# A tile of h in two VectorE operations, the next tile's product ahead of the last low part, first loads on one queue, and factors in the statistic's bank

## The chip, the cores and the metric

One NeuronCore of a Trainium2 chip runs the whole program. The metric is device time in microseconds (us) for one execution, as a median over runs. A profiled execution gives the trace. Its span, from the first to the last instruction, is a little shorter than its device time. In the profile PE is the tensor engine (PEld its weight loads), DVE is VectorE, ACT is ScalarE, POOL is GpSimd and SP is the engine that issues most of the DMAs.

## The reference: what is computed

Two layers of a decoder trunk over 512 tokens of 1024 channels, fp32 in and out. Layer 0 mixes tokens with stick-breaking attention (16 heads of 64), layer 1 with a diagonal state-space layer. After each comes a gated MLP (2 x 2816 channels) with a causal convolution of width 3. Ahead of each of these four parts stands an RMS norm whose gain and shift depend on a vector c:

```python
def rms_norm(x, g):
    y = x * lax.rsqrt(jnp.mean(x * x, axis=-1, keepdims=True) + EPS)
    return y * g

mod = silu(c) @ w_mod[i] + b_mod[i]              # 6 * 1024 numbers for a layer
sh1, sc1, g1, sh2, sc2, g2 = split(mod, 6)
h = rms_norm(x, norm_mix[i]) * (1 + sc1) + sh1   # "a tile of h" is 128 channels of this
y = attention(h)                                 # layer 0: q, k, v = split(h @ w_qkv, 3), ...
x = x + g1 * y
h = rms_norm(x, norm_ffn[i]) * (1 + sc2) + sh2
x = x + g2 * conv_ffn(h)
```

At the end stands one more such norm. In the kernel's names a tile k of h is `x[k] * rstd * a[k] + b[k]`, with `a` the gain and `b` the shift (a number for each channel, so for each partition) and `rstd` the factor of each token.

## The kernel before, in words

Channels lie on partitions and tokens along the free axis: x is eight tiles of 128 x 512. Every matrix product is made with about fp32 accuracy out of three products in a rounded format: each operand is split into a high part (rounded) and a low part (the rest), and PE makes high x high, high x low and low x high. ACT makes the high part (a copy that rounds) and DVE the low part (a difference). Weights arrive by DMA in pieces of 128 x 1024 (512 KB) in a rotating set of three raw buffers (`wraw`), and are split into a rotating set of five pairs (`wH`, `wL`).

The numbers of `mod` are products of rows of w_mod with silu(c): DVE multiplies a 128 x 1024 piece by `cact` and adds up each partition (`gemv_step`, L195), one instruction for one column of 128 numbers. Columns (1, k) are the gain of tile k and columns (0, k) its shift. The 16 columns that layer 0's first norm needs go through four slots (`slot`, `wload`, `wnext`); the others are spread over the kernel as background work.

A planner (`schedule_with_timeline_sim`) orders the instructions of each engine; `pe_pin` and `keep_in_program_order` keep the ones that they mark in the order of the code, and `follow` puts an instruction behind the last one of a line for its engine. In the first stage nearly everything is pinned.

The first stage (`attention`, the part before the score products) goes as follows.

1. First loads. `xload(0, G)`, small and `xload(1, G)` go through POOL's queue; c, the columns of w_mod, w_v and the other tiles of x through SP's.
2. v is computed before the norm's statistic is known. PE multiplies `x[k] * a[k]` (`xa_high`, `xa_low`) with w_v, and the factor of each token is applied when v leaves PSUM (`v_evict`, with the factors `yv`). v is eight banks: tiles 0 to 3 are four groups of 128 tokens for the first 512 channels, 4 to 7 the same for the second. The shift `b` can't be put in that way, so it is carried by the last token's column (`LAST`): it gets the shift instead (`shift_high`, `shift_low`), and later stages take differences of neighbouring tokens. Tiles 3 and 7 (`vz`) hold that column and wait for the shift; the six others (`va`) don't. For k below `KLATE` = 5 the products of `vz` come later, for k = 5 to 7 all eight tiles go together.
3. While this runs, squares of x are added up (`square`, `add`). After tile 7 PE sums over channels (the bank `stat`), ACT takes the root, five small DVE operations give the factors `y`. ACT and POOL make four diagonal blocks `dg` of them, and PE spreads the factors over the partitions, into a second bank (`rbc`). A copy of it is `rb`.
4. Then h itself is made, tile by tile, with `norm_tile`: on DVE `t = x * rb` (L305), on ACT the high part `a * t + b` rounded (L312) and the same affine unrounded (L314), on DVE the difference of the two (L318). Tile 0 is made between the products of k = 6 and k = 7, the others behind all of v. Evictions of v (three on DVE, `VDVE`, five on ACT) and the splits of the first k and q weights (`qk_split`) stand between the tiles.
5. PE makes k and q of head pair 0 from h, six products for each tile, then the same for pair 1, and begins with the scores (z) of pair 0. v goes out to DRAM (`sV`) and is read back one token shifted (`vs`); `v_diff` takes the difference.

A Sigmoid table is loaded on ACT, by a small activation `warm`, behind the last eviction (L805).

`norm_tile` is used three more times by way of `head_mm` (the two MLPs and the state-space layer): there in halves of 256 tokens for tiles 0 to 5 and whole for tiles 6 and 7, with the factors read from PSUM, while PE multiplies each tile with four weights at once.

Of the kernel before, what the change touches and what calls it, by code (L numbers as in the profile page):

```python
# [16 lines left out]
P = 128  # L17
# [24 lines left out]
VDVE = (1, 4, 6)  # L42
# [49 lines left out]
def _trunk(ctx, tc, I, out, tap):  # L92
# [205 lines left out]

    def norm_tile(h, k, bc, a, b, cr=FULL, pinned=False, first=None, mid=None):
        n = cr.stop - cr.start  # L300
        t = np_.tile([P, T], F32, tag="nt1", bufs=2, name="nt1")[:, :n]
        u = np_.tile([P, T], F32, tag="nt2", bufs=1, name="nt2")[:, :n]
        for part in HALF if cr == FULL and isinstance(bc, dict) else (cr,):
            src = bc[part.start] if isinstance(bc, dict) else bc
            pin["nt"] = V.tensor_tensor(t[:, part.start - cr.start:part.stop - cr.start], x[k][:, part], src[:, part], ALU.mult)  # L305
        hh, hl = h[0][k][:, cr], h[1][k][:, cr]
        hf = hh.bitcast(F32)
# [4 lines left out]
        act = S.activation(hh, t, AF.Identity, bias=b[:, k:k + 1], scale=a[:, k:k + 1])  # L312
        keep(act)
        aff = S.activation(u, t, AF.Identity, bias=b[:, k:k + 1], scale=a[:, k:k + 1])  # L314
        keep(aff)
        if mid:
            mid()
        dve = V.tensor_tensor(hl, u, hf, ALU.subtract)  # L318
        keep(dve)
        pin["head"].append([act, aff, dve])  # L320
# [218 lines left out]
    def attention(acc):  # L539
        with ExitStack() as av_, ExitStack() as ac:  # L540
# [20 lines left out]
            def xload(k, queue=SP):  # L561
                pe_pin(queue.dma_start(x[k], I["xT"][k * P:(k + 1) * P, :]))
# [24 lines left out]
            pe_pin(V.scalar_tensor_tensor(ab, sm("b_mod", mcol(0, 1, 0)), 1.0, sm("norm_mix", 0), ALU.add, ALU.mult))  # L587
# [79 lines left out]
            for i in va:  # L667
                vb[i] = bank(name=f"v{i}")
            high(0, 0)
            gv(1, 0)  # L670
            gain(0)
            xa_high(0)
            low(0, 0)
            high(0, 1)
# [4 lines left out]
            for q in TERMS:  # L679
                for half in (va[:3], va[3:]):  # L680
                    prods(0, half, (q,))
            for k in range(1, 4):
                high(k)
                gv(1, k)
                gain(k)
                xa_high(k)
                for q in (2 * k - 2, 2 * k - 1):
                    if q:
                        add(q)
                low(k)  # L690
                xa_low(k)
                for q in (2 * k, 2 * k + 1):
                    square(q)
                if k < 3:
                    prods(k, va)
            prods(3, va[:4])
            for q in (6, 7):
                add(q)
# [6 lines left out]
            prods(3, va[4:])  # L705
            high(4)
            gv(1, 4)
            nv, nsd, y, ntm = (np_.tile([P, 4], F32, tag=g, bufs=2, name=g) for g in ("nv", "nsd", "ny", "ntm"))
            pe_pin(S.activation(nsd, st[:, :4], AF.Sqrt, bias=epst, scale=1.0 / D))
            gain(4)  # L710
            xa_high(4)
# [5 lines left out]
            low(4)  # L717
            xa_low(4)
            for i in range(4):
                dst = R["dg"][:, i * P:(i + 1) * P]  # L720
                if i < 2:
                    pe_pin(S.activation(dst, ident, AF.Copy, scale=y[:, i:i + 1]))
                else:
                    G.tensor_scalar(dst, ident, y[:, i:i + 1], 0.0, ALU.mult, ALU.add)
# [7 lines left out]
            prods(4, va[:4])  # L732
            rbp = bank(aux, "rbc")
            for cr in HALF:
                pe_pin(PE.matmul(rbp[:, cr], ones, R["dg"][:, cr], start=True, stop=True))
            rb = np_.tile([P, T], F32, tag="sq", bufs=2, name="rb")
            pe_pin(S.activation(rb, rbp, AF.Copy))
            prods(4, va[4:])
            gv(0, 0)
            for i in vz:  # L740
                vb[i] = bank(aux, f"v{i}")
# [7 lines left out]
            def norm(k):  # L749
                norm_tile(h, k, rb, a, b, FULL, True)  # L750

            for k in range(KLATE, KD):
                high(k)
                gv(1, k)
                gain(k)
                xa_high(k)
                low(k)
                xa_low(k)
                gv(0, k)
                shift_high(k)  # L760
                shift_low(k)
                prods(k, va + vz)
                if k == KD - 2:
                    norm(0)
# [4 lines left out]
            def v_evict(i):  # L769
                nb, tt = divmod(i, 4)  # L770
                dst = vn[:, tt, nb * 512:(nb + 1) * 512]
                if i in VDVE:
                    pe_pin(V.tensor_scalar(dst, vb[i], yv[:, tt:tt + 1], None, ALU.mult))
                else:
                    pe_pin(S.activation(dst, vb[i], AF.Copy, scale=yv[:, tt:tt + 1]))
# [9 lines left out]
            def qk_split(nm):  # L785
                (wh, wl), qkr = qkw[0, nm]
                pe_pin(S.activation(wh, qkr, AF.Copy))
                pe_pin(V.tensor_tensor(wl, qkr, wh.bitcast(F32), ALU.subtract))
                qkw[0, nm] = wh, wl

            last_load = pin["load"]
# [10 lines left out]
            line["S"], line["V"] = pin["head"][-1][1:]  # L802
# [190 lines left out]
            for pr in range(2):  # L993
                if pr == 0:
                    for nm in QK:
                        qk_load(1, nm, True)

                    todo = []
                    units = proj(0, todo)
                    for k in range(KD):  # L1000
                        units[k]()
                        units[KD + k]()
                    for evict in todo:
                        evict()
                    for i in (1, 2, 5, 6, 3, 7, 0, 4):
                        v_diff(i, follow)
# [713 lines left out]
```

## Time and profile before

| what | before |
|---|---|
| median of 3 runs | 1197.9 us (1197.64 to 1198.16) |
| profiled execution | 1201.34 us |
| its span | 1199.3 us |
| mean granted TensorE clock | 0.996 |
| PE busy | 1164.9 us |
| DVE busy | 859.0 us |
| ACT busy | 568.8 us |
| POOL busy | 273.5 us |
| bytes moved by DMA | 211.52 MB, mean 176 GB/s |

How to read it: a row such as `62.40:93.56 31.16, 21.70 (x72) ...` gives a stretch of the span in us, its length, and for PE, PEld, DVE, ACT and POOL the busy time and the number of instructions, then the granted clock, the share of time in which the DMA engines were busy, and GB/s. A row of a timeline gives start, duration, engine, line, operation, output and inputs; in brackets stands how long the engine was idle before it and what ended that. A row of waits gives total, times and the longest one. In a row of a group the numbers behind the bar are the busy time, the mean ns of one instruction and the idle time before them. Engine times overlap, so that only a wait on the chain to the end costs time.

### The profile page before, as it was taken

What the parts mean: (1) busy time and instruction counts of PE and PEld (TensorE: products, weight loads), DVE (VectorE), ACT (ScalarE), POOL (GpSimd) and SP (SyncE); (2) the same over time, 40 slices, a digit from 0 to 9 for tenths busy, and PEclk for the clock granted to TensorE, in tenths of its full rate; (3) what the DMA queues carried; (4) which work ended last, traced back from release to release, by engine and by line L of the source; (5) the groups of instructions that cost most, each with busy time, mean ns of one, the idle gap of its engine ahead of it and who ended that gap; (6) DMA issues with size and microseconds to landing.
All of it is one profiled execution on the core that took longest, in us unless ns stands there. A gap on an engine that the chain in (4) does not pass through costs nothing.

```text
span 1199.3 us, 16512 instructions
## 1 busy us (share of the span) xinstructions
PE 1164.9 (97%) x6196; PEld 955.8 (80%) x6196; DVE 859.0 (72%) x1322; ACT 568.8 (47%) x902; POOL 273.5 (23%) x282
## 2 busy tenths in 40 slices
PE   8969999999999999999999999999999999999997
PEld 6747778679788888878888887879888888888887
DVE  6758988877799658676867598787598467744555
ACT  6466566656453134412435677645544134422443
POOL 1100111000097799979820000000000000000003
PEclk9989999999999999999999999999999999999999
DMA  9644555451157757779745598772176338442222
GB/s 362 249 158 158 158 181 162 132 183 48 49 163 250 251 167 228 225 241 296 236 144 179 180 347 275 237 238 64 51 227 211 123 118 193 145 123 71 82 77 71
DMA packets 91507, 211.52 MB, mean 176 GB/s; under 512 B 19586, under 2 KB 37778, under 8 KB 91428
## 3 DMA queue, kind: packets, MB, share of 16 engines
q1 hardware_dynamic: 78676, 192.56, 49.7%
q0 software_dynamic: 4432, 15.82, 4.2%
q10 hardware_dynamic: 8320, 2.10, 0.8%
q8 instruction: 48, 0.79, 0.3%
q14 instruction: 31, 0.25, 0.1%
HBM read 189.20 MB, written 21.24 MB: 175 GB/s over the span
## 4 chain that ended last, share of the span: by engine, by line
PE 74%; DVE 8%; issue 7%; DMA 6%; ACT 4%; POOL 1%; POOLq 0%; DVEq 0%; ACTq 0%; SPq 0%
PE up L168 13%; PE up L171 13%; PE up L172 13%; PE dn L168 6%; PE dn L171 6%; PE dn L172 6%; DMA wg<-in_w_modT_dram 3%; PE u L171 1%; PE u L168 1%; PE u L172 1%; PE wos L171 1%; PE v L661 1%; PE wo L168 1%; PE wos L172 1%; PE wo L172 1%
## 5 line engine op out<-in xcount | busy, mean ns | idle before, releaser
L168 PE MATMUL up<-hH,up_h 128*128 128x512 f32 x640 | 249.7, 391 | 0.3 <-DVE ca L458 0.3
L172 PE MATMUL up<-hH,up_l 128*128 128x512 f32 x640 | 249.2, 389 | 0.3 <-DVE up_l L163 0.3
L171 PE MATMUL up<-hL,up_h 128*128 128x512 f32 x640 | 249.2, 389 | 0.0
L458 DVE SCALAR_TENSOR_TENSOR ca<-up,small,ca 128x511 f32<-128x511 f32 (+1 forms) x176 | 131.6, 748 | 118.9 <-ACT ca L456 115.9
L168 PE MATMUL dn<-gH,dn_h 128*128 128x512 f32 (+1 forms) x394 | 146.5, 373 | 0.0
L172 PE MATMUL dn<-gH,dn_l 128*128 128x512 f32 (+1 forms) x394 | 146.0, 370 | 0.0
L171 PE MATMUL dn<-gL,dn_h 128*128 128x512 f32 (+1 forms) x394 | 145.8, 370 | 0.0
L195 DVE SCALAR_TENSOR_TENSOR wg<-wg,cact 128x1024 f32<-128x1024 f32 x96 | 120.7, 1274 | 31.7 <-DMA wg<-in_w_modT_dram 31.7
L168 PEld LDWEIGHTS up<-hH,up_h 128*128 128x128 f32 x640 | 120.1, 188 | 26.6 <-issue 1.7
L172 PEld LDWEIGHTS up<-hH,up_l 128*128 128x128 f32 x640 | 120.1, 188 | 25.7 <-DVE up_l L163 0.8
L171 PEld LDWEIGHTS up<-hL,up_h 128*128 128x128 f32 x640 | 120.1, 188 | 24.3
L456 ACT ACTIVATE ca<-up,small 128x512 f32<-128x512 f32 x88 | 68.1, 774 | 148.3 <-PE up L172 148.3
L1592 POOL TENSOR_SCALAR xa<-x,Anorm_out 128x256 f32<-128x256 f32 x7 | 5.7, 817 | 575.2 <-DVE x L352 575.2
L162 ACT ACTIVATE up_h<-up_r 128x1024 fp32r<-128x1024 f32 x80 | 84.2, 1053 | 79.7 <-PE dn L171 57.6
L163 DVE TENSOR_TENSOR up_l<-up_r,up_h 128x1024 fp32r<-128x1024 f32 x80 | 113.8, 1423 | 7.6 <-ACT up_h L162 6.8
L352 DVE SCALAR_TENSOR_TENSOR x<-dn,mod,x 128x512 f32<-128x512 f32 (+1 forms) x55 | 37.5, 681 | 79.7 <-PE dn L172 79.5
L168 PEld LDWEIGHTS dn<-gH,dn_h 128*128 128x128 f32 x394 | 73.9, 188 | 14.8 <-issue 0.6
L172 PEld LDWEIGHTS dn<-gH,dn_l 128*128 128x128 f32 x394 | 73.9, 188 | 14.2
L171 PEld LDWEIGHTS dn<-gL,dn_h 128*128 128x128 f32 x394 | 73.9, 188 | 14.2
L162 ACT ACTIVATE dn_h<-dn_r 128x1024 fp32r<-128x1024 f32 (+1 forms) x48 | 46.7, 982 | 50.5 <-PE dn L171 43.3
L474 ACT ACTIVATE gH<-gm 128x512 fp32r<-128x512 f32 x44 | 27.1, 616 | 69.8 <-DVE gm L470 69.8
L163 DVE TENSOR_TENSOR dn_l<-dn_r,dn_h 128x1024 fp32r<-128x1024 f32 (+1 forms) x48 | 59.2, 1234 | 0.4
(356 smaller groups left out, 2330.9 us busy)
## 6 DMA issues: line engine op xcount, KB each, us to landing
up_r<-in_w_up_dram SPq DMA_DIRECT2D x80, 512.0 KB
wg<-in_w_modT_dram SPq DMA_DIRECT2D x74, 512.0 KB
dn_r<-in_w_down_dram SPq DMA_DIRECT2D x32, 512.0 KB
wg<-in_w_modT_dram POOLq DMA_DIRECT2D x22, 512.0 KB, 3.8
wgs<-in_w_modT_dram SPq DMA_DIRECT2D x16, 512.0 KB
dn_r<-in_w_down_dram SPq DMA_DIRECT2D x16, 384.0 KB
wv_r<-in_w_v_dram SPq DMA_DIRECT2D x8, 512.0 KB
wk_r<-in_w_qk_dram SPq DMA_DIRECT2D x8, 512.0 KB
```

Of the source, the lines that this page charges most:

```text
L162: order("S", lambda: S.activation(wh[:, :n], raw[:, :n], AF.Copy))
L163: pin["split"] = order("V", lambda: V.tensor_tensor(wl[:, :n], raw[:, :n], wh[:, :n].bitcast(F32), ALU.subtract))
L168: ins = PE.matmul(ps, ah, bh, start=start, stop=False)
L171: PE.matmul(ps, ah, bl, start=False, stop=False)
L172: PE.matmul(ps, al, bh, start=False, stop=stop)
L195: mul = lambda: V.scalar_tensor_tensor(w, w, 1.0, cact, ALU.mult, ALU.mult, accum_out=raw[:, col:col + 1])
L352: add = lambda: V.scalar_tensor_tensor(xs, pv, gate, xs, ALU.mult, ALU.add)
L456: follow("S", lambda: S.activation(ca, ps, AF.Identity, bias=small[:, cb:cb + 1], scale=tapw[2]))
L458: follow("V", lambda: V.scalar_tensor_tensor(ca[:, q:], ps[:, :T - q], tapw[2 - q], ca[:, q:], ALU.mult, ALU.add))
L474: follow("S", lambda: S.activation(gh, m, AF.Copy))
L661: pe_pin(PE.matmul(vb[i], h[p_][k][:, tt * P:(tt + 1) * P], wv[k][q][:, nb * 512:(nb + 1) * 512], start=k == 0 and (p_, q) == (0, 0), stop ...
L1592: G.tensor_scalar(xa[k], x[k][:, cb], a[:, k:k + 1], 0.0, ALU.mult, ALU.add)
```

## The change

- `norm_tile` (all four places): the product takes the gain with it, `t = (x * a) * rstd`, one DVE instruction of the three-operand form; ACT makes one pass for the high part, `t + b` rounded; the low part is `(t + b) - high`, one DVE instruction. The unrounded affine on ACT and its buffer are gone.
- The first norm is taken out of the v loop and written as a loop of its own (`nt_mul`, `nt_high`, `nt_low`): the product of tile k + 1 stands on DVE ahead of the low part of tile k. All eight tiles come behind v's last operands. All evictions of v are on ACT, behind the high parts.
- The first loads are all on SP's queue, in the order x0, first column, small, first w_v, x1 and on. The first column's product stands ahead of `ab` on DVE.
- PE's products of one k go by term: high x high of all tiles, then high x low, then low x high; behind the last k, high x high of all tiles and then the other two terms tile by tile. Tile k = 4 comes ahead of the statistic, whose small products stand between its terms.
- The low shift of tile k stands behind the next column's product; tile 3's late products come ahead of tile 7's. For k = 5 to 7 the shift's column stands ahead of the split's low part.
- The diagonal blocks are all made on ACT; the spread factors go into the bank of the statistic (`st`), and v's tile 7 takes that bank afterwards.
- The Sigmoid table is loaded behind the splits of pair 1's weights.

The core of the diff:

```diff
     def norm_tile(h, k, bc, a, b, cr=FULL, pinned=False, first=None, mid=None):
...
-            pin["nt"] = V.tensor_tensor(t[...], x[k][:, part], src[:, part], ALU.mult)
+            pin["nt"] = V.scalar_tensor_tensor(t[...], x[k][:, part], a[:, k:k + 1], src[:, part], ALU.mult, ALU.mult)
...
-        act = S.activation(hh, t, AF.Identity, bias=b[:, k:k + 1], scale=a[:, k:k + 1])
+        act = S.activation(hh, t, AF.Identity, bias=b[:, k:k + 1])
-        aff = S.activation(u, t, AF.Identity, bias=b[:, k:k + 1], scale=a[:, k:k + 1])
...
-        dve = V.tensor_tensor(hl, u, hf, ALU.subtract)
+        dve = V.scalar_tensor_tensor(hl, t, b[:, k:k + 1], hh.bitcast(F32), ALU.add, ALU.subtract)
...
-            xload(0, G)
-            G.dma_start(small[:, :NMOD], I["small"][:, :NMOD])
-            xload(1, G)
+            xload(0)
             wload(1, 0)
+            pe_pin(SP.dma_start(small[:, :NMOD], I["small"][:, :NMOD]))
             vload(0)
+            xload(1)
             wload(1, 1)
...
+            def terms(k, tiles, qs=TERMS):
+                for q in qs:
+                    prods(k, tiles, (q,))
...
-            for k in range(1, 4):
+            for k in range(1, 5):
                 high(k)
                 gv(1, k)
                 gain(k)
                 xa_high(k)
...
                 low(k)
-                xa_low(k)
...
-                if k < 3:
-                    prods(k, va)
+                if k < 4:
+                    xa_low(k)
+                    for q in (2 * k, 2 * k + 1):
+                        square(q)
+                    terms(k, va)
...
+            terms(4, va, TERMS[:1])
             for i in range(4):
                 pe_pin(PE.matmul(st[:, i:i + 1], acc[:, i * P:(i + 1) * P], ones[:, 0:1], start=i == 0, stop=i == 3))
+            terms(4, va, TERMS[1:2])
...
+            xa_low(4)
+            terms(4, va, TERMS[2:])
...
             for k in range(KLATE):
+                gv(0, k)
+                if k == 1:
+                    for i in range(4):
+                        pe_pin(S.activation(R["dg"][:, i * P:(i + 1) * P], ident, AF.Copy, scale=y[:, i:i + 1]))
                 shift_high(k)
-                if k < KLATE - 1:
-                    gv(0, k + 1)
-                shift_low(k)
-                prods(k, vz)
+                if k:
+                    shift_low(k - 1)
+            shift_low(KLATE - 1)
+            vb[3] = bank(aux, "v3")
+            for k in range(KLATE):
+                prods(k, (3,))
+                if k == 1:
+                    for cr in HALF:
+                        pe_pin(PE.matmul(st[:, cr], ones, R["dg"][:, cr], start=True, stop=True))
+                    pe_pin(S.activation(rb, st, AF.Copy))
+            vb[7] = bank(aux, "v7")
+            for k in range(KLATE):
+                prods(k, (7,))
 
             for k in range(KLATE, KD):
                 high(k)
                 gv(1, k)
                 gain(k)
                 xa_high(k)
+                gv(0, k)
+                shift_high(k)
                 low(k)
                 xa_low(k)
-                gv(0, k)
-                shift_high(k)
                 shift_low(k)
-                prods(k, va + vz)
-                if k == KD - 2:
-                    norm(0)
+                if k < KD - 1:
+                    terms(k, va + vz)
+                else:
+                    terms(k, va + vz, TERMS[:1])
+                    for i in va + vz:
+                        terms(k, (i,), TERMS[1:])
...
-            norm(1)
             ev = list(va + vz)
-            for q, k in enumerate(range(2, KD)):
-                v_evict(ev.pop(0))
-                if q < 2:
-                    qk_split(QK[q])
-                norm(k)
-            for i in ev:
-                v_evict(i)
+            nt_mul(0)
+            for k in range(KD):
+                nt_high(k)
+                if k < 2:
+                    qk_split(QK[k], True)
+                nt_mul(k + 1)
+                if k < 2:
+                    qk_split(QK[k], False)
+                nt_low(k)
+                for q in range((0, 2, 1, 1, 1, 1, 1, 1)[k]):
+                    v_evict(ev.pop(0))
...
-            warm = np_.tile([P, 64], F32, tag="warm", bufs=1, name="warm")[:, 0:1]
-            pe_pin(S.activation(warm, ones[:, 0:1], AF.Sigmoid))
...
                     for nm in QK:
                         qk_load(1, nm, True)
+
+                    warm = np_.tile([P, 64], F32, tag="warm", bufs=1, name="warm")[:, 0:1]
+                    follow("S", lambda: S.activation(warm, ones[:, 0:1], AF.Sigmoid))
```

More of the change, by code (lines that the diff above doesn't have):

```diff
@@ L41 @@
 KLATE = 5
-VDVE = (1, 4, 6)
 USTG = (6, 7)
@@ L586, in attention @@
             b = mod[:, 0:KD]
-            pe_pin(V.scalar_tensor_tensor(ab, sm("b_mod", mcol(0, 1, 0)), 1.0, sm("norm_mix", 0), ALU.add, ALU.mult))
             def gv(v, k):
@@ L668, in attention @@
                 vb[i] = bank(name=f"v{i}")
+            def terms(k, tiles, qs=TERMS):
+                for q in qs:
+                    prods(k, tiles, (q,))
             high(0, 0)
             gv(1, 0)
+            pe_pin(V.scalar_tensor_tensor(ab, sm("b_mod", mcol(0, 1, 0)), 1.0, sm("norm_mix", 0), ALU.add, ALU.mult))
             gain(0)
             xa_high(0)
+            high(0, 1)
             low(0, 0)
-            high(0, 1)
             low(0, 1)
@@ L678, in attention @@
             square(1)
-            for q in TERMS:
-                for half in (va[:3], va[3:]):
-                    prods(0, half, (q,))
-            for k in range(1, 4):
+            terms(0, va)
+            for k in range(1, 5):
                 high(k)
@@ L716, in attention @@
             pe_pin(V.scalar_tensor_tensor(y, ntm, 1.5, y, ALU.add, ALU.mult))
[L717 to L724, printed above, removed]
             yv = np_.tile([P, 4], F32, tag="yv", bufs=1, name="yv")
@@ L771, in v_evict @@
                 dst = vn[:, tt, nb * 512:(nb + 1) * 512]
[L772 to L775, printed above, removed]
+                pe_pin(S.activation(dst, vb[i], AF.Copy, scale=yv[:, tt:tt + 1]))
             qkw = {}
```

59 lines of the change are left out of this document (24 added, 35 removed).

## The prediction

> **What bounds the kernel now.** I read the head of the page first, then the busy time by stage, then what the tensor engine waited for, then the chain and the groups of the stage that the change rewrites.
>
> ```profile
> span 1199.3 us, 16512 instructions
> PE 1164.9 (97%) x6196; PEld 955.8 (80%) x6196; DVE 859.0 (72%) x1322; ACT 568.8 (47%) x902; POOL 273.5 (23%) x282
> ...
> core 0: us, PE busy (x) PEld busy (x) DVE busy (x) ACT busy (x) POOL busy (x), PEclk, DMA share, GB/s
> 11.47:34.35 22.88, 21.94 (x95) 16.43 (x94) 20.86 (x34) 15.14 (x26) 4.77 (x5) 1.00 0.92 356
> 34.35:62.40 28.05, 26.44 (x113) 20.48 (x111) 19.56 (x36) 14.96 (x32) 0.47 (x3) 1.00 0.68 241
> 62.40:93.56 31.16, 21.70 (x72) 14.47 (x73) 17.70 (x24) 20.28 (x29) 0.00 (x0) 0.89 0.56 187
> 93.56:122.00 28.44, 25.99 (x133) 20.09 (x134) 24.46 (x38) 16.74 (x34) 1.68 (x3) 1.00 0.43 144
> 276.00:300.00 24.00, 24.00 (x187) 23.07 (x186) 17.24 (x43) 19.29 (x34) 0.00 (x0) 1.00 0.17 47
> 654.00:678.00 24.00, 23.79 (x177) 22.47 (x176) 19.24 (x51) 19.25 (x34) 0.00 (x0) 1.00 0.48 179
> ```
>
> PE is busy for 97% of the span, and in the later heads (276 and 654 us are the rows of two of three) nearly without a gap. Time can therefore be had only where PE waits, and what is won there moves all later PE work forward. The poor row is 62.40 to 93.56, from the last v product to the first score product z.
>
> ```profile
> 11.47 1.61 PE L661 MATMUL v<-wv_h,hH 128*128 128x512 f32 x6
> 45.60 0.39 PE L661 MATMUL v<-wv_h,hL 128*128 128x512 f32 x1
> 54.44 0.39 PE L661 MATMUL v<-wv_h,hL 128*128 128x512 f32 x1
> 87.20 0.50 PE L168 MATMUL k<-hH,wk_h 128*128 128x512 f32 x1 [1.47 <-ACT wk_h L162]
> 93.56 0.36 PE L887 MATMUL z<-kA,q_sq 128*128 128x256 f32 x1
> ```
>
> From 45.60 to 54.44 lie 40 products, 39 steps: 0.2267 us each. Between 11.47 and 93.56 PE has 264 of them (192 of v, 48 of pair 0's k and q, 24 of pair 1's k), 59.9 us, and two small blocks of about 0.95 us (statistic, factors). That is 61.8 us of work in 82.1 us: 20.3 us are lost, and some 15 of them after 62.40 (31.16 less 72 x 0.2267). The chain there repeats one figure, tile after tile:
>
> ```profile
> 71.35 0.61 DVE nt L305
> ...
> 71.99 0.82 ACT hH L312
> 72.81 0.72 ACT nt L314
> 73.55 0.69 DVE hL L318
> ...
> L312 ACT ACTIVATE hH<-nt,mod,Amix 128x512 fp32r<-128x512 f32 x8 | 6.5, 814 | 11.4 <-DVE nt L305 11.4
> L314 ACT ACTIVATE nt<-nt,mod,Amix 128x512 f32<-128x512 f32 x8 | 6.4, 800 | 0.0
> L633 DVE SCALAR_TENSOR_TENSOR hL<-x,Amix,hH 128x512 fp32r<-128x512 f32 x8 | 6.1, 766 | 0.2
> L318 DVE TENSOR_TENSOR hL<-nt,hH 128x512 fp32r<-128x512 f32 x8 | 5.5, 692 | 12.8 <-ACT nt L314 12.8
> ```
>
> A tile of h is product on DVE, two affines on ACT, difference on DVE, one behind the other: 0.61 + 0.82 + 0.72 + 0.69 = 2.84 us, because DVE starts the next product only after this difference. PE needs 6 x 0.2267 = 1.36 us per tile. DVE and ACT are each idle half the time: a latency, not a load.
>
> **The later v tiles and the norm.** In the new order no norm is made inside the v loop. Per k = 5 to 7 DVE has two column products, one split, one low part and a small difference:
>
> ```profile
> L195 DVE SCALAR_TENSOR_TENSOR wgs<-wgs,cact 128x1024 f32<-128x1024 f32 x16 | 19.5, 1223 | 0.0
> L612 DVE TENSOR_TENSOR wv_l<-wv_r,wv_h 128x1024 fp32r<-128x1024 f32 x7 | 8.5, 1219 | 0.0
> L775 ACT ACTIVATE vn<-v,yv 128x512 f32<-128x512 f32 x5 | 3.2, 666 | 0.0
> L630 ACT ACTIVATE hH<-x,Amix 128x512 fp32r<-128x512 f32 x8 | 5.8, 724 | 0.3
> ```
>
> 2 x 1.30 (with its 0.08 read) + 1.22 + 0.77 + 0.16 = 4.75 us by durations, some 4.4 when each successor starts 0.07 before the end of the last (the chain counts 0.61 for a product of 0.68). PE has 24 x 0.2267 = 5.44 us. PE leads; the products by terms let the high ones start before the low parts exist.
>
> The tile of h becomes two fused DVE operations and one ACT operation. The nearest row to both fused ones is L633, same shape and inputs, 0.766; the lower end is the plain 0.69, the upper a half-speed 1.38. I take 0.77. DVE from its last shift: 16 x 0.77 + 2 x 1.22 (splits of wk, wq) = 14.8 us by durations, 13.5 with the overlaps. ACT: eight high parts (0.72 as for a gain alone, 0.81 at most), eight evictions of 0.67 (three come from DVE), two splits of 1.04: 13.2 to 13.9 us. DVE's last shift comes at about 51 and PE's last v product at 57.7 (both below). So the last low part is there at 64.5 to 65.8, and PE, continuous, wants it at 57.7 + 7 x 1.36 = 67.2: a margin of about 2 us. PE's waits for hL, hH, wk and the eviction of v go; pair 0 takes 10.9 us instead of 23.
>
> Pair 1 then follows at once: today PE waits 1.47 us for wk_h because ACT loads a table and warms it first (1.28 + 0.20 us). The table moves behind the two splits, where ACT has about a microsecond before the k bank is complete; gone if it lands before the evictions, else up to 1.5 us of the z start.
>
> **The first loads.** Times before:
>
> ```profile
> 1.29 0.74 POOL L562 DMA_DIRECT2D x<-in_xT_dram  x1 [0.35 <-issue]
> 5.27 1.06 ACT L1546 ACTIVATE cact<-crow 128x1024 f32<-128x1024 f32 x1 [3.03 <-DMA crow<-in_c_dram]
> 8.69 0.17 DVE L587 SCALAR_TENSOR_TENSOR ab<-small 128x8 f32<-128x8 f32 x1 [7.68 <-DMA small<-in_small_dram]
> 8.81 1.23 DVE L195 SCALAR_TENSOR_TENSOR wgs<-wgs,cact 128x1024 f32<-128x1024 f32 x1
> 9.37 0.63 ACT L608 ACTIVATE wv_h<-wv_r 128x512 fp32r<-128x512 f32 x1 [3.04 <-DMA wv_r<-in_w_v_dram]
> 12.78 1.06 ACT L608 ACTIVATE wv_h<-wv_r 128x1024 fp32r<-128x1024 f32 x1
> 16.69 1.06 ACT L608 ACTIVATE wv_h<-wv_r 128x1024 fp32r<-128x1024 f32 x1 [0.20 <-DMA wv_r<-in_w_v_dram]
> ```
>
> Between crow (5.27) and wv0 (9.37) lie wg0 and wv0 on SP and up to 596 KB on POOL's queue, about 1620 KB in 4.1 us. On one queue the order is x0 256, wg0 512, small 84, wv0 512 KB, then x1: pro rata, wg0 at 7.2, small at 7.4, wv0 at 8.7. The column product no longer stands behind ab, which follows it at 8.6. The first v product was 2.1 us behind wv0, so it comes at 10.8, 0.67 us earlier (0 if the queue is no faster so, 1.5 if the column was the limit). SP issues three DMAs more, at 0.4 to 0.65 us each, in front of all later loads; the bytes ahead of wv1 and wv2 stay the same, so these do not land earlier (12.78, 16.69). wv1's split, gain and high part end at 12.78 + 1.06 + 0.39 + 0.72 = 14.95, where PE has done 18 products at 14.9; for wv2 the same sum gives 18.9 against 19.1. From there PE waits for nothing in k = 2 and 3, since by the terms order the low part is needed only 12 products behind the first one; k = 4 starts at 27.3, and the statistic behind its six high products ends at 29.6.
>
> **The late shifts.** After the statistic come a root and five small DVE operations, about 1.2 us; then DVE makes five columns in a row, from 30.8 to 37.3, and the low shift of k waits for column k+1. The fifth is through at about 37.8; three times 4.4 behind it DVE is at the 51 used above. Tile 3's fifteen products follow that pace and end at 38.0, tile 7's at 41.4; without it PE would be there at 40.1 (29.6 + 42 products + 0.95). Loss 1.3 us. Factors in the statistic's bank cost nothing unless the copy rb is late: it stands on ACT behind all five shifts, done by about 37.7, and tile 7's first product waits for it. Three v tiles of 5.44 us then end at 57.7.
>
> **The sum.** First product 10.8 + work 61.8 + 0.1 (k = 1) + 1.3 (late shifts) = z at 74.0, from 93.56: -19.5. Then:
> - behind z, ACT waits 3.3 us for the next wq, which PE feels as 2.1 us of waits for om; its load starts when wk's split frees the buffer, at about 66, and lands near 73 with today's 6.6 us, where ACT wants it at 72. I count -0.5, between -2.1 and 0.
> - the columns on the five shifts want 512 KB every 1.2 us, 437 GB/s, where the first stage's 356 at a share of 0.92 give 387 at full: +0.5, up to +3.
> - v's round trip through memory and four weight loads fall into about 20 us instead of 33: +0.5, up to +3.
>
> ```profile
> 89.22 6.63 DMA wq_r<-in_w_qk_dram
> ...
> ACT wq_h L162 <- DMA wq_r<-in_w_qk_dram: 3.3, 1, 3.3
> ...
> PE z L887 <- ACT om L892: 2.1, 2, 1.6
> PE u L171 <- DVE hL L318: 0.2, 1, 0.2
> ```
>
> Heads: per head 14 products and 14 low parts become fused. From PSUM the product rises to the 0.48 us of the residual's fused form, the low part by the ratio 766/692: 14 x 0.115 = +1.6 us of DVE (19.24 to 20.8 of 24), ACT loses 14 affines. PE's only wait on them is 0.2 us. I count 0, within 0.2 of it.
>
> ```profile
> 655.22 0.42 DVE L318 TENSOR_TENSOR hL<-nt,hH 128x256 fp32r<-128x256 f32 x1
> 655.56 0.41 DVE L305 TENSOR_TENSOR nt<-x,rbc 128x256 f32<-128x256 f32 x1
> 654.80 0.48 DVE L352 SCALAR_TENSOR_TENSOR x<-dn,mod,x 128x256 f32<-128x256 f32 x1 [0.42 <-PE dn L172]
> ```
>
> Net -19.0. The profiled execution took 1201.34 us (span 1199.3, 2.0 around it), so 1182.3; it lies 3.4 above the median 1197.9. Against the median: 1178.9, said as 1179.
>
> **Rivals.**
> - Loads late. Both DMA terms near their upper ends: -13 to -15, 1183 to 1188. For it: DMA is at 0.92 in the first stage and the second would rise from 0.68. Against: PE's list of waits names no load in this stretch.
> - Given back after z. DVE is busy 24.46 of 28.44 us behind z, with the scans and the differences of v; PE's 2.45 us of gaps there could grow by the 5 us of v's differences if v's round trip is late: 1184 to 1189.
> - The fused operation is slow. With 1.38 us for two SBUF sources, the stage needs 16 x 1.38 + 2.4 = 24.5 us of DVE, the last low part comes at 75 and PE wants it at 67.2, and the low parts of a head add 14 x 0.43 = 6 us, which fills DVE to 24 of 24: 1187 to 1191. Row L633 at 0.766 speaks against it. [...]
> - Hidden anyway. z stays near its time since the next pair's weights or v's round trip set it: 1195.5 to 1200. Against: those loads start at buffers that come free earlier too.
> - Slower. In the three heads DVE becomes the bound and PE waits for every low part. To eat 19 us a head must lose 6.4, so DVE must need 30.4 us where it has 17.2 to 19.2 in 24: a tile's two operations at about 1.7 us instead of 0.95. From there on it is slower; 1200 to 1206.
>
> **How the numbers follow.** Likeliest, PE fed from 10.8 to 74 and little given back: 0.64, its own range 1176 to 1183. Loads late 0.17; given back 0.08; slow form 0.03; hidden 0.03; slower 0.03; more than 22 us gained 0.02. The range 1174 to 1188 holds the first, the second and half of the third. Faster by over 0.2% (2.4 us, about what a measurement of this kernel tells from no change) 0.94, within 0.03, slower 0.03.
>
> **What would show it.** Right: first v product near 10.8; no PE wait for hL, hH or an eviction after the last v product, which ends near 58; k and q of pair 0 at 0.2267 us; z near 74; fused tile operations at 0.75 to 0.8 us, 0.48 in the heads. Wrong: column products waiting for their load between 31 and 42; ACT on the chain with eviction after high part; PE waiting for wk, wq or om behind 68; a PE wait for hL of more than a microsecond in a head.

## The result and the profile after

The changed kernel takes 1186.58 us (median of 4 runs, 1185.91 to 1187.3) against 1198.03 for the kernel before on the same chip: a ratio of 0.9897, 95% interval 0.9876 to 0.9919, or 11.45 us less. The profiled execution after is the one of 1185.91 us.

First the head of the page after, then the busy time by stage. The stages are cut at the first v product, at 34.35 as before, at the first k product and at the first z; the last row is as long as the one behind z before. Columns as before.

```profile
span 1184.1 us, 16460 instructions
PE 1159.9 (98%) x6196; PEld 956.9 (81%) x6196; DVE 864.5 (73%) x1319; ACT 538.5 (45%) x857; POOL 271.5 (23%) x277
...
10.61:34.35 23.74, 23.26 (x102) 18.26 (x103) 21.94 (x38) 16.91 (x32) 3.81 (x4) 1.00 1.01 389
34.35:58.72 24.37, 24.34 (x103) 19.14 (x104) 21.37 (x36) 15.28 (x30) 0.23 (x2) 1.00 0.76 269
58.72:75.67 16.95, 16.48 (x73) 13.33 (x71) 13.59 (x19) 14.29 (x21) 0.00 (x0) 1.00 0.79 256
75.67:104.46 28.79, 23.72 (x112) 18.59 (x113) 22.82 (x35) 14.76 (x29) 1.83 (x3) 0.94 0.50 161
```

Up to z PE now has almost no gap. The poor row has moved: it is the one behind z, with 5.1 us of PE idle in 28.8 and a granted clock of 0.94. PE's timeline shows the marks of the first stage and that gap:

```profile
10.61 0.74 PE L656 MATMUL v<-wv_h,hH 128*128 128x512 f32 x2 [0.34 <-ACT hH L625]
42.40 0.84 PE L656 MATMUL v<-wv_h,hH 128*128 128x512 f32 x3
58.72 0.39 PE L167 MATMUL k<-hH,wk_h 128*128 128x512 f32 x1
75.67 0.38 PE L893 MATMUL z<-kA,q_sq 128*128 128x256 f32 x1 [0.47 <-DVE q_sq L875]
84.96 0.46 PE L893 MATMUL z<-kA,q_sq 128*128 128x384 f32 x1 [4.75 <-ACT om L898]
86.18 0.63 PE L167 MATMUL q<-hH,wq_h 128*128 128x512 f32 x1
86.60 0.63 PE L170 MATMUL q<-hL,wq_h 128*128 128x512 f32 x1
```

z comes 17.89 us earlier than the 93.56 of before. But 9.3 us after it PE starts again from a stop of 4.75 us, and then the 128x512 products follow each other at 0.42 to 0.43 us instead of 0.23, with a granted clock of 0.54 from 84.96 to 88.71. The reason for the stop is in SP's queue and in ACT's timeline:

```profile
71.47 3.26 SPq L828 DMA_DIRECT2D vs<-sV  x4
74.77 0.43 SPq L159 DMA_DIRECT2D wq_r<-in_w_qk_dram  x1
...
67.80 1.22 DVE L162 TENSOR_TENSOR wk_l<-wk_r,wk_h 128x1024 fp32r<-128x1024 f32 x1 [0.77 <-ACT wk_h L161]
81.12 1.06 ACT L161 ACTIVATE wq_h<-wq_r 128x1024 fp32r<-128x1024 f32 x1 [6.41 <-DMA wq_r<-in_w_qk_dram]
```

The raw buffer of the next wq is free when wk's split ends (67.80 + 1.22 = 69.02). Its load is issued only at 74.77, because it stands in SP's queue behind four reads of v (71.47 to 74.73), and SP's reads wait for v's writes: 8.8 us in five waits between 60 and 80 us. ACT stands 6.41 us at the split, and the evictions that z needs stand behind it. PE's list of waits after has this entry on top, and two that the list before lacks, the high parts of the heads (up: both MLPs, u: state-space layer):

```profile
PE z L893 <- ACT om L898: 4.8, 1, 4.8
...
PE up L167 <- ACT hH L310: 2.2, 2, 1.1
...
PE u L167 <- ACT hH L310: 1.1, 1, 1.1
```

To see where time is won and lost later, take the first product of six kinds from PE's timelines: z, o (with v, pair 0), dn (first MLP), pv (state-space core), glu (the gated product behind it, the first with the weights wgl) and fin (the last norm). Stretches in us, in the profiled executions of all kernels told of here:

| kernel | z at | z to o | o to dn | dn to pv | pv to glu | glu to fin |
|---|---|---|---|---|---|---|
| before | 93.56 | 22.91 | 254.43 | 316.39 | 69.35 | 433.57 |
| after | 75.67 | 26.84 | 254.10 | 317.36 | 66.85 | 433.90 |
| e1 wq early | 75.57 | 21.78 | 256.14 | 317.97 | 70.66 | 434.49 |
| e2 old heads | 75.22 | 26.64 | 251.81 | 316.11 | 69.21 | 433.05 |
| e3 before, new heads | 95.39 | 20.68 | 254.67 | 318.84 | 66.95 | 434.30 |
| e4 no look-ahead | 81.68 | 25.82 | 252.47 | 317.77 | 69.90 | 434.35 |
| e5 first loads back | 76.06 | 27.92 | 251.21 | 317.52 | 66.82 | 434.47 |
| e6 norm stage alone | 79.92 | 27.23 | 252.23 | 316.04 | 66.83 | 433.32 |
| e7 e1 and e2 | 75.53 | 21.85 | 253.08 | 316.22 | 66.85 | 433.17 |
| e8 v differences on POOL | 75.18 | 24.78 | 254.99 | 316.04 | 67.36 | 433.10 |
| e9 heads in old order | 75.54 | 27.39 | 250.19 | 316.17 | 66.88 | 432.13 |
| e10 e9 and wq early | 75.80 | 21.74 | 253.76 | 316.18 | 69.01 | 433.51 |
| e11 v differences late | 75.29 | 28.81 | 249.44 | 316.44 | 70.58 | 432.97 |

Read the two first rows: -17.89 at z, +3.93 to o, -0.33 to dn, +0.97 to pv, -2.50 to glu, +0.33 to fin, together the -15.49 by which fin comes earlier. The column pv to glu has two values in all kernels, about 66.9 and 69 to 70.7. The longer ones go with one wait, here in the kernel before, which the kernel after doesn't show (pB is a piece that the state-space core reads back from memory):

```profile
PE pv L1375 <- DMA pB<-sB: 2.2, 1, 2.2
```

It is 1.6 to 2.2 us in before, e1, e2, e4, e10 and e11, 0.3 in e8 and absent in the others, e3 with the old first stage among them. Kernels with and without the change are on both sides, so the 2.5 us at this place are most likely not the change's.

The column o to dn holds two waits that differ between the kernels. One is in the first head, 1.1 us for hH, in after, e1, e3, e4 and e5. The other is that of the output projection wo for oL, the low part of its input: 1.7 us in after, 1.5 in before, 0.6 to 1.8 in e1, e3, e4, e8 and e10, and absent in the rest. No run tells what brings it: e5, which differs from after in three loads at the start alone, doesn't have it.

### The profile page after: what moved, and what is told of

Its sections match the earlier page's. It is cut to its first block, busy times and chain, and to the rows that moved or that the text cites. A ratio compares the mean times of both kernels' runs of the same rounds, so it can differ in the third digit from the quotient of the medians.

```text
span 1184.1 us, 16460 instructions
## 1 busy us (share of the span) xinstructions
PE 1159.9 (98%) x6196; PEld 956.9 (81%) x6196; DVE 864.5 (73%) x1319; ACT 538.5 (45%) x857; POOL 271.5 (23%) x277
## 4 chain that ended last, share of the span: by engine, by line
PE 81%; DVE 6%; issue 6%; DMA 3%; ACT 2%; POOL 1%; SPq 0%; POOLq 0%; DVEq 0%; ACTq 0%
PE up L167 14%; PE up L170 14%; PE up L171 14%; PE dn L167 7%; PE dn L171 7%; PE dn L170 7%; DMA wg<-in_w_modT_dram 2%; PE v L656 2%; PE u L167 1%; PE u L170 1%; PE u L171 1%; PE wos L170 1%; PE wo L167 1%; PE wos L171 1%; PE wo L171 1%
## 5 line engine op out<-in xcount | busy, mean ns | idle before, releaser
L161 ACT ACTIVATE up_h<-up_r 128x1024 fp32r<-128x1024 f32 x80 | 84.2, 1053 | 80.7 <-PE dn L170 66.9
```

What stands on the lines that cost most here:

```text
L161: order("S", lambda: S.activation(wh[:, :n], raw[:, :n], AF.Copy))
```

## The experiments

Times are medians; ratios are to the kernel before, run on the same chip.

**e1: one load on another queue.** In the changed kernel wq of pair 2 goes through POOL's queue.

```diff
-                qk_load(2, nm)
+                qk_load(2, nm, queue=G if nm == "q" else SP)
```

> The changed kernel with one load moved: wq of pair 2 is issued on POOL's queue instead of SP's, where it stood behind the writes of v and their shifted reads and was issued at 74.8 us, though its buffer was free at about 69. Every other queue keeps its order. Theory A (the gain given back behind z is this load's place in SP's queue): it is issued near 69, lands near 76, ACT's 6.4 us wait and PE's 4.75 us wait for om go, and with them the slower products behind that gap: about 1181.5 us, 4 to 6 below the changed kernel's 1186.6. Rival B (DVE is full there with the differences of v and the scans, so another wait takes the place of this one): at most 1.5 us gained, 1185 to 1187. Rival C (the memory system is full, so the load lands near 80 wherever it is issued): 1185 to 1187, with the wait for wq still above 4 us.

Measured: 1182.61 us, 0.9874 (0.9852 to 0.9896). POOL's and ACT's timelines and PE's waits between 75 and 130 us:

```profile
69.22 0.75 POOL L159 DMA_DIRECT2D wq_r<-in_w_qk_dram  x1 [34.60 <-DVE wk_l L162]
...
75.75 1.06 ACT L161 ACTIVATE wq_h<-wq_r 128x1024 fp32r<-128x1024 f32 x1 [1.14 <-DMA wq_r<-in_w_qk_dram]
...
PE t L911 <- DVE om L899: 1.9, 3, 1.0
```

The load is issued 5.55 us earlier, lands before 75.75, and the wait for om is gone: theory A in its mechanism, and 4.0 us by the medians. The size is rough: the two intervals overlap, and the profiled execution is the slowest of the six, 1188.11 us, itself no faster than the changed kernel. The table shows 5.1 us won from z to o and 2.0 given back up to dn, where PE now waits more for the scans (t for om, 2.8 us in the whole execution against 1.1 after). Rival C falls, B holds for a part.

**e2 and e3: the form of a tile in the heads.** e2 is the changed kernel with the old `norm_tile` in the heads, e3 the kernel before with the new one there.

```diff
 e2, in norm_tile (its callers are the three heads alone)
-   V.scalar_tensor_tensor(t, x, a, src), S.activation(hh, t, bias=b), V.scalar_tensor_tensor(hl, t, b, hh)
+   V.tensor_tensor(t, x, src), S.activation(hh, t, b, a), S.activation(u, t, b, a), V.tensor_tensor(hl, u, hh)
 e3: the same in reverse, in head_mm of the kernel before
```

> The changed kernel, but in the three heads a tile is made as before (product on DVE, two affines on ACT, difference on DVE); the first norm keeps the new form. Theory A (the new form costs a head 1 to 2 us, since PE waits for the high part of the second half, 2.2 us in the MLPs and 1.1 in the state-space layer by the list of waits): 1182 to 1184, and these waits for hH are gone. Rival B (the form is neutral in the heads and the shifts seen there are the planner's other order of PE's work, which evens out): 1186 to 1188.

> The kernel before with the new form of a tile in the three heads alone; the first norm and the whole first stage stay as before. Theory A (the form costs a head 1 to 2 us): 1201 to 1203 against 1198.0, with waits of PE for hH in the heads. Rival B (neutral): 1197.5 to 1199. Rival C (the form alone helps the heads, since 14 affines of ACT go): 1195 to 1197.

Measured: e2 1183.91 us, 0.9874 (0.9854 to 0.9893), 2.7 below the changed kernel; e3 1201.88 us, 1.0034 (1.002 to 1.0048), 3.2 above the kernel before. In e2 PE's list of waits has no entry for hH in the heads, in e3 it has the same two as after, 2.2 and 1.1. Theory A in both directions: with the new form the heads cost about 3 us. By the table the state-space head (dn to pv) and the last one (glu to fin) pay, 1.25 and 0.85 in e2; the first head lies in the stretch from o to dn.

**e9: the new form with PE's old order in the heads.** The two products that the second half's factors come from are held ahead of tiles 3 and 5 (HEADS moves the place of the first one in the code to tile 2).

```diff
+   late = {HEADK - 3: "stat", HEADK - 1: "rbc"}.get(k) if cr == HALF[0] else None
+   with tc.issue_after(pin[late].ins) if late else ExitStack():
        mm3(ps[:, cr], wk(w, k), ...)
-HEADS = (1, 2)
+HEADS = (2, 3)
```

> The changed kernel, new form of a tile everywhere, with PE's order in the heads held as it stands with the old form: the statistic of the second half ahead of tile 3's products, the spread factors (rbc) ahead of tile 5's, by putting those products behind them in the order of issue. In the changed kernel both stand later, rbc behind tile 5's products, so that nothing covers the product on DVE and the high part on ACT. Theory A (the heads lose by this order, which the planner chooses for the faster tiles, not by the form): the 1.1 us waits of PE for hH go in all three heads, and the time is that of the kernel with the old form in the heads, 1183 to 1184.5. Rival B (the form itself is dearer, DVE being later with each tile): the waits move to hL or rbc and the time stays at 1186 to 1187.

Measured: 1181.55 us, 0.9852 (0.9834 to 0.987), below theory A's band. PE's timeline in the first head, the changed kernel's three rows first, then e9's two, then a stretch of 24 us of that head after and in e9:

```profile
270.95 0.50 PE L262 MATMUL stat<-ones,acc 128*128 128x1 f32 x4
274.84 0.59 PE L284 MATMUL rbc<-dg,ones 128*128 128x256 f32 x2
276.55 0.74 PE L167 MATMUL up<-hH,upo_h 128*128 128x256 f32 x4 [1.11 <-ACT hH L310]
...
267.30 0.50 PE L262 MATMUL stat<-ones,acc 128*128 128x1 f32 x4
270.61 0.59 PE L284 MATMUL rbc<-dg,ones 128*128 128x256 f32 x2
...
265.80:289.80 24.00, 22.89 (x172) 21.67 (x171) 16.38 (x38) 9.30 (x17) 0.00 (x0) 1.00 0.21 67
263.00:287.00 24.00, 24.00 (x178) 22.86 (x177) 16.27 (x38) 9.30 (x17) 0.00 (x0) 1.00 0.24 67
```

After, rbc comes when all tiles of the first half are used up; the product on DVE and the high part on ACT then stand bare, and PE waits 1.11 us. In e9 twelve products of tile 5 cover them, and PE works 24.00 of 24 us with the same DVE and ACT work. So the heads paid for the order that the planner chose with the new form, not for the form's own operations: theory A in its mechanism. (Why the planner chose it, no run shows.) By the table e9 is 1.19 (dn to pv) and 1.77 (glu to fin) faster than after, and 3.91 from o to dn. There the 1.1 us of the first head are gone, and the wait of wo for oL, 1.7, as well, which is not the heads'. Without that wait the 5.0 us between the medians come to 3.3, close to the 3 of e2 and e3.

**e4: no look-ahead.** Undoes one part: the product of tile k + 1 stands behind the low part of tile k.

```diff
-                nt_mul(k + 1)
                 if k < 2:
                     qk_split(QK[k], False)
                 nt_low(k)
+                nt_mul(k + 1)
```

> The changed kernel without the look-ahead: the product of tile k + 1 stands on DVE behind the low part of tile k. Theory A (it is the latency of a tile that held PE, and the look-ahead is what hides it): a tile then takes about 0.67 + 0.72 + 0.70 = 2.1 us, the last low part comes near 69.5 and not 66.3, PE wants it at 67.4 and waits about 2 to 3 us for hL and hH between 60 and 71; z comes 2 to 3 us later: 1188 to 1190, unless the late wq load (74.8 us), which sets the end behind z, hides all of it: then 1186 to 1187. Rival B (the fusion alone is enough, since 2.1 us a tile begin well ahead of PE): z stays at 75.7 and the time at 1186 to 1187.5, without waits for hL.

Measured: 1192.03 us, 0.994 (0.9923 to 0.9957); z at 81.68. DVE's timeline, and one row of ACT's:

```profile
63.39 0.75 DVE L795 SCALAR_TENSOR_TENSOR hL<-nt,mod,hH 128x512 fp32r<-128x512 f32 x1 [0.79 <-ACT hH L791]
64.06 0.75 DVE L788 SCALAR_TENSOR_TENSOR nt<-x,Amix,rb 128x512 f32<-128x512 f32 x1
65.60 0.75 DVE L795 SCALAR_TENSOR_TENSOR hL<-nt,mod,hH 128x512 fp32r<-128x512 f32 x1 [0.79 <-ACT hH L791]
...
64.84 0.72 ACT L791 ACTIVATE hH<-nt,mod 128x512 fp32r<-128x512 f32 x1 [0.91 <-DVE nt L788]
```

A tile takes 65.60 - 63.39 = 2.21 us, PE needs 1.36 and waits for hL in six tiles. Pair 0's products take 15.9 us (58.43 to 74.36) instead of 10.9; with 0.8 more of the wait for q_sq and 0.4 in pair 1, less a start 0.3 earlier, that makes the 6.0 that z loses. Theory A, with its size too small: it had 1188 to 1190 and the last low part near 69.5; that one starts at 72.29, 6.0 later than after. The products of the first three tiles start at 51.06, 55.35 and 59.65, so that the first two tiles take 4.3 us each, with the split of a weight in between. The late load hides only 1.0 of it. Without the look-ahead the change brought 6.7 us on this chip, a little over half.

**e5: the first loads as before** (x0, small and x1 on POOL's queue).

```diff
+            xload(0, G)
+            G.dma_start(small[:, :NMOD], I["small"][:, :NMOD])
+            xload(1, G)
-            xload(0)
             wload(1, 0)
-            pe_pin(SP.dma_start(small[:, :NMOD], ...))
             vload(0)
-            xload(1)
```

> The changed kernel with x0, small and x1 back on POOL's queue, the first columns' loads on SP as before. Theory A (the order on one queue brings the first column and w_v forward): the first v product comes at 11.3 to 11.5 instead of 10.61, k = 1 starts 0.4 to 0.8 later than 14.96 and z as much later than 75.67; time about 1187, too little for the time alone to show, so the start times decide. Rival B (the second w_v, which arrives at 12.8 either way, sets k = 1): k = 1 and z do not move; time 1186.6. Rival C (SP, relieved of three issues, brings all later loads forward): k = 2 starts before 19.1 and z comes up to 1 us earlier.

Measured: 1186.24 us, 0.9886 (0.9862 to 0.991). The first v product:

```profile
11.64 2.10 PE L656 MATMUL v<-wv_h,hH 128*128 128x512 f32 x6
```

It is 1.03 us later than after, a little more than theory A has, and k = 1 is 1.36 later (16.32 against 14.96). But k = 5 and z are only 0.39 later (42.79 and 76.06): in between, the kernel after waits 0.67 us for a column's load, and e5 catches up. Theory A for the place, not for z; the time shows nothing.

**e6: the norm stage alone.** The kernel before with the loop of `nt_mul`, `nt_high`, `nt_low`, all evictions on ACT and the table moved; front and heads as before.

```diff
-            norm(1)
...
+            nt_mul(0)
+            for k in range(KD):
+                nt_high(k) ... nt_mul(k + 1) ... nt_low(k) ... v_evict
```

> The kernel before with the second stage of the change alone: the first norm in its own loop behind v, with the two fused operations and the look-ahead, all evictions on ACT, the table behind pair 1's splits. First loads, the order of v's terms, the late shifts, the second bank and the form of a tile in the heads stay as before. Theory A (most of what was won up to z is the norm's latency, the front gives the rest): v's last product stays at 62 or comes a little earlier, the k and q products run without a wait, z comes at 78.5 to 80 (14 us earlier than 93.56); behind z some 4 us are given back as in the changed kernel: 1187 to 1190 against 1198. Rival B (the front is worth half): z at 82 to 85, 1191 to 1194. Rival C (the stage alone is worth all of it, as the late wq load then sets the end behind z in both): 1184 to 1187.

Measured: 1186.51 us, 0.989 (0.9869 to 0.9912), as fast as the whole change. PE's and SP's timelines:

```profile
79.92 0.39 PE L897 MATMUL z<-kA,q_sq 128*128 128x256 f32 x1 [1.31 <-DVE q_sq L879]
...
79.13 0.43 SPq L160 DMA_DIRECT2D wq_r<-in_w_qk_dram  x1
```

z comes at 79.92, as theory A has it; the time is in rival C's band, but not by C's mechanism: the wq load here is later by 4.36 us too, and at o e6 is still 4.64 behind the changed kernel. Up to o the front is worth that much. The new order in the heads spends most of it: e2, which has the front and the old heads, has a median 2.6 us below e6's, on another chip and with intervals that overlap.

**e7, e10, e8, e11: put together.** e7 is e1 with e2's heads, e10 is e1 with e9's order. e8 is e7 with four of the eight differences of v on POOL; e11 is e10 with four of them on DVE behind pair 0's scans.

```diff
 e8
-   order("V", lambda: V.tensor_tensor(dst, dst, vs[i], ALU.subtract))
+   G.tensor_tensor(dst, dst, vs[i], ALU.subtract)        # i in (3, 7, 0, 4)
 e11
+   window(0, proj(1), FILL0)
+   with tc.issue_after(pin["scan"].ins):
+       for i in (3, 7, 0, 4): v_diff(i, free2)
```

> The changed kernel with pair 2's wq on POOL's queue and the tile of h as before in the three heads. Theory A (the two costs lie in different places and add): 4.0 from the load and 2.7 from the heads off 1186.6, that is 1179 to 1181. Rival B (what the two won is largely the same slack, used up at a later wait of the attention stage): 1181.5 to 1184.

> The kernel of the run before this one (wq on POOL's queue, old form in the heads) with four of the eight differences of v made by POOL instead of DVE. With the wq load out of the way PE was seen to lose 1.5 us near 96 and 1.9 near 115 to the scans on DVE (waits t for om). Theory A (DVE's load right behind z is what gives that back): 2.4 us less work on DVE there, 1 to 3 us faster than the run without it. Rival B (those waits follow from the columns' loads, behind which DVE waits 2.4 and 1.0 us near 95, so that the scans behind them are late anyway): within 1 us of it. Rival C (POOL is slow at these differences and the product with v waits for them): slower.

> The run before this one with pair 2's wq on POOL's queue as well. Theory A (waits in different places): as the kernel with that load and the old form in the heads, 1181.3, within 1.5 us. Rival B (the new form is the better one once its order is right, since ACT has 14 affines less): 1177 to 1179.5. Rival C (the two shares overlap): 1182.5 to 1184.

> The run before this one with the last four differences of v on DVE behind pair 0's scans instead of ahead of them. With the wq load early, DVE was without a gap from 73 to 91 us, and PE waited for the scans (t for om). Theory A (DVE's order there gives back a part of what the early load wins): the scans end 2.5 us earlier, the differences still end some 3 us ahead of the first product with v (98 us), and 1 to 2.5 us are won: 1179 to 1180.5 if the run before stands at 1181.3. Rival B (the time is set by the third pair's scans behind the columns' loads near 95 and 115): within 0.7 us of the run before.

Measured: e7 1181.27 us, 0.9843 (0.9819 to 0.9867); e10 1181.73, 0.9846 (0.9827 to 0.9865); e8 1184.12, 0.9873 (0.9851 to 0.9896); e11 1182.59, 0.986 (0.9841 to 0.9879). e7 lies between its two bands. e10 has the number of its theory A, but e9 alone had it already, so that the early load shows no gain there: it wins 5.65 from z to o and loses 3.57 from o to dn (2.3 us of waits for the scans there, 0.5 in e9, and 0.7 for oL), and the two medians can't be told apart. Moving the differences didn't help in either way; e11 lies in neither of its bands. e8, DVE's groups between 74 and 90 us and POOL's row; last e7's group for the same work:

```profile
L840 DVE TENSOR_TENSOR vn<-vn,vs 128x512 f32<-128x512 f32 x4 | 5.8, 1508 | 0.0
L162 DVE TENSOR_TENSOR wq_l<-wq_r,wq_h 128x1024 fp32r<-128x1024 f32 x1 | 2.3, 2318 | 0.0
...
76.06 6.78 POOL L838 TENSOR_TENSOR vn<-vn,vs 128x512 f32<-128x512 f32 x4 [6.45 <-DMA vs<-sV]
...
L837 DVE TENSOR_TENSOR vn<-vn,vs 128x512 f32<-128x512 f32 x8 | 5.0, 687 | 0.1
```

DVE took longer for four differences beside POOL's four (5.8 us) than for all eight in e7 (5.0), and the split behind them 2.32 us instead of 1.22. The kernel is slower, as in rival C, but through DVE and not by a wait for POOL. In e11 the first two scans come sooner (81.17, in e10 84.00), but not the six behind them (85.96 and 85.77), and the planner put the differences and two columns ahead of q's low part:

```profile
91.07 2.47 DVE L835 TENSOR_TENSOR vn<-vn,vs 128x512 f32<-128x512 f32 x4
93.46 1.22 DVE L194 SCALAR_TENSOR_TENSOR wg<-wg,cact 128x1024 f32<-128x1024 f32 x1
...
96.60 0.58 PE L895 MATMUL z<-kA,q_sq 128*128 128x256 f32 x1 [4.41 <-DVE q_sq L877]
```

A new wait of 4.41 us takes the place of the one attacked. Best are e7, e9 and e10, some 5 us below the changed kernel; which of the three is ahead the runs can't say.

## Why the prediction was right or wrong, point by point

The time, 1186.58, is inside the range of 1174 to 1188, and the sign is right. It is 7.6 us above the forecast of 1179 and outside the likeliest case's own range; it lies in the bands of two rivals, "loads late" and "given back after z". The mechanism is mostly the second one's, PE's gaps behind z, though through a load stuck in a queue and not through v's differences. So the range holds the result because it took in these rivals; the forecast's own saving of 19.0 us is too large by 6.0, in the places listed below. Two of its signs of being wrong came true: a wait for om behind 68 us, and a column that waited for its load between 31 and 42.

- **What bounded the kernel: right.** A tile's latency, not a load. e6 shows the norm stage alone to bring 13 us on its chip, e4 that taking the look-ahead away from the whole change costs 5.4.
- **The fused operations: right.** Forecast 0.77 us; DVE's and ACT's groups between 50 and 68 us after:

```profile
L795 DVE SCALAR_TENSOR_TENSOR hL<-nt,mod,hH 128x512 fp32r<-128x512 f32 x8 | 6.0, 746 | 0.2 <-ACT hH L791 0.2
L788 DVE SCALAR_TENSOR_TENSOR nt<-x,Amix,rb 128x512 f32<-128x512 f32 x8 | 5.9, 749 | 0.2
L791 ACT ACTIVATE hH<-nt,mod 128x512 fp32r<-128x512 f32 x8 | 5.8, 722 | 4.1 <-DVE nt L788 3.8
```

  0.746 and 0.749 against 0.692 for the plain difference: 8% more. The rival of the slow form falls: its 1.38, twice the plain difference's 0.69, was an upper end that no tile of h in the profile after shows.
- **The front: right within 0.2 us.** First v product forecast 10.8, measured 10.61; e5 shows that only 0.39 of that 1 us reaches z.
- **Late shifts and columns' loads: too small.** k = 5 was to start at 41.4 and starts at 42.40. One column waited 0.67 us for its load at 35.09, the term that stood with +0.5. v ends 1.0 later than forecast.
- **k and q of pair 0: right.** 58.72 to 69.60 is 10.88, forecast 10.9, without a wait.
- **The table: open.** PE waits 0.47 us for q_sq at z, within the 1.5 allowed; whether the table is the cause, no run shows. With the 1.0 us of the late shifts this makes most of the 1.67 by which z misses 74.0.
- **The next wq: the step that failed.** I had its load start "when wk's split frees the buffer, at about 66". The buffer was free at 69.02, 3 us later than that, and the load then stood in SP's queue behind v's reads until 74.77. The term had -0.5 between -2.1 and 0, and the wait of PE grew from 2.1 to 4.8 us, with 1.7 more for the ten slow products behind it. I moved v's writes earlier and did not ask who is queued behind their round trip on SP. SP's timeline before had it already: wk's split ended at 88.40, and the load followed the four reads at 89.22.

```profile
86.91 2.27 SPq L822 DMA_DIRECT2D vs<-sV  x4
89.22 0.43 SPq L160 DMA_DIRECT2D wq_r<-in_w_qk_dram  x1
```

  e1 shows it: another queue, and the wait is gone. What that is worth in time is less sure: 4.0 us by e1's median, 2.6 from e2 to e7 on two chips, nothing from e9 to e10.
- **The heads: wrong.** Counted as 0 within 0.2. They cost 2.7 to 3.2 us (e2, e3), and the wait is for hH, not for hL. Not for the reason that I priced (DVE's longer operations: 16.27 us of DVE in 24 with PE full in e9), but because in the planner's new order the spread factors stand behind the last cover (e9).
- **The sum.** By the table: 17.9 won at z where 19.5 were forecast; +3.6 from z to dn where the three terms made +0.5; +1.3 in the two later heads' stretches where 0 stood. That leaves 13.0, and with the 2.5 of the state-space wait the 15.5 between the profiles. Setting the saving against the median of 1197.9 and not the profile's 1201.34 was sound: the wait of 2.2 us for pB in that profile may be a part of the 3.4 between them, and none of the saving was counted there. The 1.5 us between 13.0 and the 11.45 of the medians stay open; the wait for oL alone comes to as much.

## What to carry to other kernels

Where a stage is pulled forward, list for each queue what is issued behind the steps that move, and give each load the time at which its queue gets to it (74.77 for the next wq here), not that at which its buffer is free (69.02). Where a planner orders instructions by its own costs, a change of an operation's form can move a small product that others wait for behind its cover: compare the order, and pin those. A chain that goes to and fro between two engines wants the next item's first step ahead of this item's last one; without that the change brought a little over half (6.7 us in e4).

## What the runs showed of the hardware

- DVE's differences of two SBUF tiles took longer beside POOL's: in e8 DVE made four from 75.88 to 81.68 us and POOL four from 76.06 to 82.84, at 1.51 us each on DVE and 1.72 on POOL, against 0.69 on DVE in e7, where it makes all eight. Four of each took 7.0 us together, and DVE's four 5.8 against 2.5 in e11. (What POOL's take with DVE idle, and why DVE's took longer, no run shows.)
- Behind the gap of 4.75 us PE was slow for 3.75 us: from 84.96 to 88.71 the granted clock was 0.54 and its 128x512 products came at 0.42 to 0.43 us each. From 75.67 to 80.21, ahead of the gap, and again from 88.71 to 92 it was 1.00, and they came at 0.23. In e11, behind the wait of 4.41 us, they came at 0.42 to 0.43 as well (97.98 to 98.83). (What links the two, and from what length of a gap, no run shows.)
- The read-back pB is late in the profiles of some of these kernels and not of others, whatever their first stage, and those take 2 to 4 us longer from pv to glu (69.0 to 70.7 against 66.8 to 67.4). There is one profile of each kernel, so that no run shows whether one program has both.
